# Interleaving the high and low parts of the up weights and moving the activations to another byte offset in a one-core hybrid decoder layer

## The chip, the cores and the metric

The kernel runs on one NeuronCore of a Trainium2 chip. The metric is the device time of one execution in microseconds (us). The core has a matrix engine (TensorE, PE in the profile, its weight loads PEld), VectorE (DVE), ScalarE (ACT), GpSimd (POOL) and a queue that issues transfers (SP). They share a memory of 128 partitions, SBUF; TensorE writes into eight banks of a second one, PSUM.

## The reference, cut to what matters

```python
h = rms_norm(x, mix_norm)
z = h @ w_in                           # q, k, v, r, gate of group A; q, k, v of group B
o_gla = silu(gr) * rms_norm(gla_chunked(gq, gk, gv, log_a), gla_norm)
o_swa = swa_sink_attention(sq, sk, sv, sinks)
x = x + concat([o_gla, o_swa]) @ w_out
h2 = rms_norm(x, ffn_norm)
u = causal_dwconv(h2 @ w_up, conv_w, conv_b)       # 3 taps along the sequence
a, b = split(u, 2)
x = x + (silu(a) * b) @ w_down
```

Sequence and model width are 1,024, the inner width of the feed-forward part is 2,816. All is float32.

## The kernel before, in words

**Precision.** A float32 matrix is split into a high part `hi`, rounded to the format of TensorE's fast float32 mode, and a low part `lo = x - hi`. A product is three fast matmuls: high by high, high by low, low by high (`PASSES`, line 30). `split` (line 95) makes the parts: ScalarE copies the high part, and GpSimd or VectorE subtracts it from the source for the low part. A matmul takes a stationary operand of 128 columns (the weight load) and streams a moving operand of up to 512 columns against it.

**Tiles.** `big` (line 65) holds the transposed activations, high and low: 65,536 bytes in each partition. In the dense stage it is the stationary operand, in the up stage the moving one. Its order before is half of the sequence, block of 128 features `k`, part `r`, row block within the half, row: `rows(t, ks, r)` takes the rows of one block `t`, and `b_operand` (line 810) takes all 512 rows of a half, which then lie in one run of 2,048 bytes. `ex` (line 667) holds three sums of activations in the same way. Weights lie in slots of 4,096 bytes (`slot_tile`, line 85), high part in the first 2,048 bytes, low part in the second.

**Stages.** First come five dense products with `w_in` (`dq`, `dk`, `dv`, `dg`, `dr`) with the attention work between them, then the product with `w_out` (`do`); `dense` (line 323) issues 24 matmuls for a row block (eight blocks of features, three passes), except that `unit_q_part` (line 710) issues those of the first three `dq` row blocks in pieces. Then the feed-forward part runs over 22 chunks of 128 inner columns. Each chunk makes seven up products P1 to P7 of a Strassen-like scheme (`product`, line 830), 12 matmuls each: the weights are the stationary operand, `big` (P1, P2, P3, P5) or `ex` (P4, P6, P7) the moving one. `up_operand` (line 788) makes the weights of each, `post` the convolution taps and the gate, and between the up products run the down products of the chunk pair before (`down_pair`, line 1014), whose two operands both lie in slots.

**Order.** A list of events with due times, written out by hand at the end of the function, sets the order of the program; each engine works through its own queue in that order. Weights of an up product are made two products ahead.

**Where the tiles lie.** The memory map of this kernel gives, in bytes of each partition: `big` from 1,152, `cc` (convolution constants, 704 bytes) from 66,688, three raw buffers from 67,392, `acc` from 79,680, `ex` from 112,448. From the other end: `mhalf` (96 bytes) from 229,248, nine slots below it from 192,384 on, 4,096 bytes apart. Small tiles take a multiple of 32 bytes.

Of the kernel before, what the change touches and what calls it, by code (L numbers as in the profile page):

```python
# [9 lines left out]
F32 = mybir.dt.float32  # L10
F32R = mybir.dt.float32r
# [6 lines left out]
P = 128  # L18
T = 1024
D = 1024  # L20
NT = T // P
KD = D // P
# [12 lines left out]
def hymba_layer_kernel(ctx, tc, x, mix_norm, w_in, w_alpha2, b_alpha, gla_norm,  # L35
# [3 lines left out]
    act, dve, pool, pe, sp = nc.scalar, nc.vector, nc.gpsimd, nc.tensor, nc.sync  # L39
# [10 lines left out]
    base = ctx.enter_context(tc.tile_pool(name="base", bufs=1))  # L50
# [4 lines left out]
    def bank(name):  # L55
        ps["n"] += 1
        if "f" in ps:
            return ps["f"][2 + ps["n"] % 2]

        for start, which in (("n2pt_6", "b"), ("do1_7", "a"), ("n2pt_3", "a")):  # L60
            if name.startswith(start):
                return ps[which].tile([P, 512], F32, tag="b", name=name)
        return ps["ab"[ps["n"] % 2]].tile([P, 512], F32, tag="b", name=name)

    big = base.tile([P, 2, KD, 2, 4, P], F32R, name="big")

    def rows(t, ks, r):
        return big[:, t // 4, ks, r, t % 4, :]

    RAW_BUFS, K4, K2, N_WARM = 3, 6, 5, 5  # L70

# [1 line left out]
        return base.tile([P, 1024], F32, tag="raw", name=name, bufs=RAW_BUFS)  # L73

    edge = ctx.enter_context(tc.tile_pool(name="edge", bufs=1, side="right"))
    mhalf = edge.tile([P, 24], F32, name="mhalf")
    w_keep = ctx.enter_context(tc.tile_pool(name="wa", bufs=1, side="right"))
    w_late = {}
    swp = ExitStack()
# [5 lines left out]
    def slot_tile(slot, name, dt=F32R):  # L85
        return w_keep.tile([P, 2, 512], dt, tag=f"w{slot}", name=name, bufs=1)
# [8 lines left out]
    def split(src, hi, lo, eng=None, hi_eng=None):  # L95
        if hi_eng is None:
            act.copy(hi, src)  # L97
        else:
            hi_eng.tensor_copy(hi, src)
        (eng or pool).tensor_sub(lo, src, hi.bitcast(F32))  # L100
# [126 lines left out]
    def norm2_sums(t):  # L227

        i, ex, pn = t - 4, fin["ex"], fin["pn"]
        p0, p1 = fin["pb", t]  # L230

        def put(src, hi, lo):
            split(src, hi, lo, dve)

        def extra(n):
            return ex[:, n, :, 0, i, :], ex[:, n, :, 1, i, :]

        def own(ks):
            return rows(t, ks, 0), rows(t, ks, 1)

        b12 = pn.tile([P, 4, P], F32, tag="b12", name=f"b12_{t}", bufs=1)
        b11, b21 = ([rows(i, ks, r).bitcast(F32) for r in range(2)] for ks in (slice(0, 4), slice(4, 8)))
        act.copy(b12, p0)
        put(p1, *own(slice(4, 8)))
        dve.tensor_sub(p0, p0, b11[0])
        dve.tensor_sub(p0, p0, b11[1])
        put(p0, *own(slice(0, 4)))
        dve.tensor_sub(p1, p1, b12)
        put(p1, *extra(1))
        dve.tensor_add(p1, p1, b11[0])  # L250
        dve.tensor_add(p1, p1, b11[1])
        put(p1, *extra(0))
        dve.tensor_sub(p0, b21[0], p1)
        dve.tensor_add(p0, p0, b21[1])
        put(p0, *extra(2))

    trs = {}

    def tr_hi(t, q, h, tag):
        pt = bank(f"{tag}pt_{t}_{q}")  # L260
        for k in range(4):
            c = (q * 4 + k) * P
            pe.transpose(pt[:, k * P:(k + 1) * P], h[:, c:c + P], ident)
        trs[tag, t, q] = pt.rearrange("p (k c) -> p k c", k=4)
        act.copy(rows(t, slice(q * 4, q * 4 + 4), 0), trs[tag, t, q])

    def tr_lo(t, q, tag):
        hi, lo = (rows(t, slice(q * 4, q * 4 + 4), r) for r in range(2))
        dve.tensor_sub(lo, trs[tag, t, q], hi.bitcast(F32))

    def norm_tr(t, h, tag):
# [5 lines left out]
    blocks = {}  # L277
# [45 lines left out]
    def dense(t, ws, n, name):  # L323
        pb = bank(name)
        for k in range(KD):
            for i, (ra, rb) in enumerate(PASSES):
                pe.matmul(pb[:, :n], lhsT=rows(t, k, ra), rhs=ws[k][:, rb, :n],  # L327
                          start=(k == 0 and i == 0), stop=(k == KD - 1 and i == 2))
        return pb

# [299 lines left out]
    def gate_tr(t, gs):  # L630
        pb = bank(f"ogt{t}")
        for h in range(4):
            pe.transpose(pb[:, h * P:(h + 1) * P], gs[:, h * P:(h + 1) * P], ident)
        pv = pb.rearrange("p (h c) -> p h c", h=4)
        hi, lo = (rows(t, slice(0, 4), r) for r in range(2))
        act.activation(hi, pv, AF.Copy, scale=glan)
        dve.scalar_tensor_tensor(lo, pv, glan, hi.bitcast(F32), op0=ALU.mult, op1=ALU.subtract)
        src = qo[:, t, :].rearrange("p (j c) -> p j c", j=4)
        hi, lo = (rows(t, slice(4, 8), r) for r in range(2))
        split(src, hi, lo)  # L640


    fin = {}
# [19 lines left out]
    def open_norm2():  # L663
        st.close()
        w_late["pool"] = swp.enter_context(tc.tile_pool(name="wb", bufs=1, side="right"))
        xp = ctx.enter_context(tc.tile_pool(name="xp", bufs=1))
        fin["ex"] = xp.tile([P, 3, 4, 2, 4, P], F32R, name="ex")
        fin["sn"] = ExitStack()
        pn = fin["pn"] = fin["sn"].enter_context(tc.tile_pool(name="pn", bufs=1))
        ffn = fin["ffn"] = pn.tile([P, D], F32, name="ffn")  # L670
        sp.dma_start(ffn, ffn_norm.partition_broadcast(P).rearrange("p o d -> p (o d)"))
        fin["s1"] = pn.tile([P, 4, P], F32, name="s1_0")
# [18 lines left out]
    psb = {}  # L691
# [18 lines left out]
    def unit_q_part(t, k0, k1):  # L710
        if k0 == 0:
            psb["q", t] = bank(f"dq{t}")
        pb = psb["q", t]
        for k in range(k0, k1):

            for i, (ra, rb) in enumerate(((0, 0), (1, 0), (0, 1))):
                pe.matmul(pb, lhsT=rows(t, k, ra), rhs=blocks["q"][k][:, rb, :],  # L717
                          start=(k == 0 and i == 0), stop=(k == KD - 1 and i == 2))

    def q_done(t):  # L720
# [2 lines left out]
    def unit_q(t):  # L723
        q_post(t, dense(t, blocks["q"], 512, f"dq{t}"))

    def unit_k(t):
        kvl_post(t, dense(t, blocks["k"], 272, f"dk{t}"))

    def unit_v(t):
        act.activation(vg[0][:, t, :], dense(t, blocks["v"], 512, f"dv{t}"), AF.Copy, scale=row_scale(t))  # L730
# [14 lines left out]
        if half == 1:  # L745
            norm2_stat(t)


    cc = base.tile([P, 4, 44], F32, name="cc")

    def conv_cols():
        cr = k2_tile("cr")[:44, :].rearrange("p (j c) -> p j c", j=4)
# [24 lines left out]
    def sums(s1, a11, a21, a22, eng=pool):  # L777
        eng.tensor_add(s1, a21, a22)
        eng.tensor_sub(a21, a11, a21)
        eng.tensor_sub(a11, s1, a11)  # L780
# [7 lines left out]
    def up_operand(ch, name):  # L788
        ra, rb = raws["u", ch, 0], raws.get(("u", ch, 1), raws["u", ch, 0])
        a11, a12, a21, a22 = ra[:, 0:4], ra[:, 4:8], rb[:, 0:4], rb[:, 4:8]  # L790
        src = {"A11": a11, "A12": a12, "A21": a21, "A22": a22, "S2": a11, "S3": a21,
               "S4": a11 if ch else a12}.get(name)
        if name == "S2" and ch:
            s1 = psb["S1", ch] = fin["ff"].tile([P, 4, P], F32, tag="s", name=f"S1_{ch}", bufs=1)
            sums(s1, a11, a21, a22)
        elif name == "S1":
            src = psb["S1", ch]
        elif name == "S4" and ch:
            pool.tensor_sub(a11, a12, a11)
        slot = U_SLOT.get((ch, name))  # L800
        if slot is None:
            slot = 1 + -turn[0] % 3
            turn[0] += 1
            U_SLOT[ch, name] = slot
        w = fin["pn"].tile([P, 2, 512], F32R, name=f"{name}w_{ch}") if slot < 0 else slot_tile(slot, f"{name}w_{ch}")
        w = w.rearrange("p r (k n) -> p r k n", k=4)
        split(src, w[:, 0], w[:, 1], dve if ch < 2 and name[1] == "1" and name[0] == "A" else None)
        blocks["u", ch, name] = w

    def b_operand(name, k, r):  # L810
        ex = fin["ex"]
        return {"B11": big[:, 0, k, r], "B21": big[:, 0, 4 + k, r],
                "B22": big[:, 1, 4 + k, r], "T1": big[:, 1, k, r],
                "T2": ex[:, 0, k, r], "T3": ex[:, 1, k, r], "T4": ex[:, 2, k, r]}[name]

    PROD = {"P1": ("A11", "B11"), "P2": ("A12", "B21"), "P3": ("S4", "B22"), "P4": ("A22", "T4"),
            "P5": ("S1", "T1"), "P6": ("S2", "T2"), "P7": ("S3", "T3")}
# [77 lines left out]
        act.copy(dst, pb)  # L895

    def save_edge(ch, key, pb):
        e = psb[key, ch] = fin["ff"].tile([P, 2], F32, tag="e", name=f"{key}_{ch}", bufs=2)
        act.copy(e, pb[:, 510:512])

    def c11(ch):
        pb = psb["P2", ch]
        dve.tensor_add(pb, psb["p1", ch], pb)
        ua = psb["ua", ch] = wide_tile(f"ua{ch}", "ua")
        conv(ch, 0, ua, pb, 0, 512, True)
        save_edge(ch, "e", pb)
# [191 lines left out]
    for c in halves:  # L1098
        split(mix_row[:, c], mix_hl[0][0:1, c], mix_hl[1][0:1, c], dve)
        pb = bank(f"mix{len(mix_ps)}")  # L1100
# [119 lines left out]
    for ch, i, name in order:  # L1220
# [7 lines left out]
        if ch < 2 or (ch, i) == (2, 0):  # L1228
            n = 0
        elif ch < L - 1 or (ch, i) == (L - 1, 0):  # L1230
            n = 1
        else:
            n = 2
# [24 lines left out]
    for p in range(NPAIR):  # L1258
        for k in range(7):

            n = 7 * p + k - 2
# [51 lines left out]
```

## Time and profile before

| what | value |
|---|---|
| median of 3 runs | 1039.2 us (1038.97 to 1039.4) |
| the profiled execution | 1039.1 us |
| its span, first to last instruction | 1037.4 us |
| granted TensorE clock | 1.000 |
| busy: PE, DVE, ACT, POOL | 99%, 76%, 46%, 60% |
| the chain that ended last | PE 97% |

The profile is one execution recorded by the hardware. A group row of it names line, engine, operation, what it writes and reads (`out<-in`), shape and count, then busy time in us, the mean duration in ns, and the idle time before with what ended it. A timeline row has its start and its length in us, then the same names and the count of equal instructions that it merges. A row of the windows view has, after the stretch, the busy time and count of PE, PEld, DVE, ACT and POOL, then the granted clock and the transfers. Matmuls are pipelined, so a single one's duration is longer than the step from one to the next.

### The profile page before, as it was taken

How to read it: one execution, taken by the hardware profiler on the slowest of the kernel's cores; microseconds unless marked ns; L12 is line 12 of the kernel's file. 1: busy time of each engine (PE TensorE's matmuls, PEld its weight loads, DVE VectorE, ACT ScalarE, POOL GpSimd, SP SyncE). 2: the span in 40 equal slices, each digit the busy share in tenths (PEclk: the TensorE clock that was granted, in tenths of full speed). 3: DMA queues.
4: the chain of work that ended last, by engine and by line, in shares of the span. 5: the costliest groups of instructions: out<-in, count | busy, mean ns of one | idle time of the engine just before them, and what ended most of it. 6: DMA issues, size and time to landing. Idle time of an engine off the chain costs nothing.

```text
span 1037.4 us, 13921 instructions
## 1 busy us (share of the span) xinstructions
PE 1030.0 (99%) x4976; PEld 849.3 (82%) x4976; DVE 793.4 (76%) x1332; ACT 480.6 (46%) x988; POOL 618.4 (60%) x510
## 2 busy tenths in 40 slices
PE   9999999999999999999999999999999999999998
PEld 6899887888888888888888888888888888888887
DVE  6776667755131699887979899897979798998976
ACT  5627655445340446554444445444444444454441
POOL 4592132325550205867868787877778787978750
PEclk9999999999999999999999999999999999999999
DMA  6152113002044202112120111222121211121104
GB/s 217 61 154 62 45 50 93 21 1 82 1 122 163 61 1 82 41 41 82 41 81 26 57 45 57 61 62 62 41 82 41 62 41 47 55 62 61 41 21 162
DMA packets 67502, 67.13 MB, mean 65 GB/s; under 512 B 4648, under 2 KB 52201, under 8 KB 67434
## 3 DMA queue, kind: packets, MB, share of 16 engines
q1 hardware_dynamic: 63448, 61.27, 18.9%
q10 hardware_dynamic: 3986, 4.99, 2.0%
q8 instruction: 39, 0.64, 0.2%
q14 instruction: 29, 0.24, 0.1%
HBM read 57.33 MB, written 4.19 MB: 59 GB/s over the span
## 4 chain that ended last, share of the span: by engine, by line
PE 97%; DMA 1%; DVE 1%; ACT 0%; issue 0%; POOL 0%; DVEq 0%; ACTq 0%; SPq 0%
PE fb L843 39%; PE dn_P L1024 18%; PE do L327 8%; PE dr L327 4%; PE dg L327 4%; PE dv L327 4%; PE dq L327 3%; PE dk L327 2%; PE gb L843 2%; PE dq L717 1%; PE pv L500 1%; PE fb L1053 1%; PE dl L1053 1%; PE go L610 1%; PE ga L601 1%; PE sc L453 1%
## 5 line engine op out<-in xcount | busy, mean ns | idle before, releaser
L1028 DVE TENSOR_TENSOR acc<-acc,dn_P 128x1024 f32<-128x1024 f32 x140 | 169.9, 1215 | 61.5 <-PE dn_P L1024 60.3
L1024 PE MATMUL dn_P<-dw,dg 128*128 128x512 f32 x840 | 214.0, 390 | 0.0
L1024 PEld LDWEIGHTS dn_P<-dw,dg 128*128 128x128 f32 x840 | 157.6, 188 | 34.5
L327 PE MATMUL do<-wow,big 128*128 128x512 f32 x384 | 90.9, 393 | 0.0
L100 POOL TENSOR_TENSOR dw<-dn,dw 128x512 fp32r<-128x512 f32 x50 | 68.8, 1376 | 25.3 <-ACT dw L97 24.1
L327 PEld LDWEIGHTS do<-wow,big 128*128 128x128 f32 x384 | 71.1, 188 | 14.4
L895 ACT COPY ca<-fb 128x512 f32<-128x512 f32 x62 | 36.3, 586 | 68.2 <-PE fb L843 68.2
L843 PE MATMUL fb<-ex,S2w 128*128 128x512 f32 x252 | 62.5, 394 | 0.0
L843 PE MATMUL fb<-ex,S3w 128*128 128x512 f32 x252 | 62.5, 394 | 0.0
L850 DVE SCALAR_TENSOR_TENSOR ua<-fb,cc,ua 128x511 f32<-128x511 f32 x84 | 62.2, 741 | 0.3
L843 PE MATMUL fb<-ex,A22w 128*128 128x512 f32 x252 | 62.2, 394 | 0.0
L843 PE MATMUL fb<-big,A11w 128*128 128x512 f32 x252 | 61.2, 389 | 0.0
L843 PE MATMUL fb<-big,S1w 128*128 128x512 f32 x252 | 61.1, 389 | 0.0
L843 PE MATMUL fb<-big,S4w 128*128 128x512 f32 x252 | 61.1, 389 | 0.0
L843 PE MATMUL fb<-big,A12w 128*128 128x512 f32 x252 | 60.9, 390 | 0.0
L843 PEld LDWEIGHTS fb<-ex,S2w 128*128 128x128 f32 x252 | 47.2, 187 | 11.3
L843 PEld LDWEIGHTS fb<-ex,A22w 128*128 128x128 f32 x252 | 47.2, 187 | 11.3
L843 PEld LDWEIGHTS fb<-ex,S3w 128*128 128x128 f32 x252 | 47.2, 187 | 11.3
L843 PEld LDWEIGHTS fb<-big,S1w 128*128 128x128 f32 x252 | 47.3, 188 | 10.0
L843 PEld LDWEIGHTS fb<-big,A11w 128*128 128x128 f32 x252 | 47.3, 188 | 10.0
L843 PEld LDWEIGHTS fb<-big,S4w 128*128 128x128 f32 x252 | 47.3, 188 | 10.0
L843 PEld LDWEIGHTS fb<-big,A12w 128*128 128x128 f32 x252 | 47.2, 188 | 9.8
(432 smaller groups left out, 2392.1 us busy)
## 6 DMA issues: line engine op xcount, KB each, us to landing
up<-in_w_up_dram SPq DMA_DIRECT2D x44, 512.0 KB, 3.8
dn<-in_w_down_dram SPq DMA_DIRECT2D x22, 512.0 KB, 3.5
acc<-in_x_dram SPq DMA_DIRECT2D x8, 512.0 KB, 6.5
out_dram<-acc SPq DMA_DIRECT2D x15, 256.0 KB, 2.0
xt<-in_x_dram SPq DMA_DIRECT2D x7, 512.0 KB, 3.2
vraw<-in_w_in_dram SPq DMA_DIRECT2D x4, 512.0 KB, 3.9
graw<-in_w_in_dram SPq DMA_DIRECT2D x4, 512.0 KB, 3.7
qt<-qt ACTq DMA_DIRECT2D x16, 128.0 KB, 2.2
```

What stands on the lines that cost most here:

```text
L100: (eng or pool).tensor_sub(lo, src, hi.bitcast(F32))
L327: pe.matmul(pb[:, :n], lhsT=rows(t, k, ra), rhs=ws[k][:, rb, :n], start=(k == 0 and i == 0), stop=(k == KD - 1 and i == 2))
L453: pe.matmul(pbs[-1][:, j % 2, :], lhsT=ql[:, g, qc], rhs=kt[:, g, kc], start=False, stop=True)
L500: pe.matmul(pbs[i][HALF[g]], lhsT=vv[rows, t - 1 + b, HALF[g]], rhs=rhs[rows, :, HALF[i]], start=start, stop=stop)
L601: pe.matmul(pb[:, pr * 256:(pr + 1) * 256], lhsT=gqt[t][:, pr, :], rhs=qbd[t % 2][:, pr], start=(pr == 0), stop=(pr == 1))
L610: pe.matmul(pb[:, h * P:(h + 1) * P], lhsT=asb[:, h, :], rhs=v[:, h * P:(h + 1) * P], start=(h == 0), stop=(t == 0 and h == 3))
L843: pe.matmul(pb, lhsT=w[:, ra, k, :], rhs=b_operand(bn, k, rb), start=(onto is None and i == 0), stop=(i == 11), skip_group_check=onto is n ...
L850: dve.scalar_tensor_tensor(dst, src, w, dst, op0=ALU.mult, op1=ALU.add)
L895: act.copy(dst, pb)
L1024: pe.matmul(pb[:, i], lhsT=g[:, ra, c:c + P], rhs=w[:, rb, :], start=(onto is None and n == 0), stop=(n == 2), skip_group_check=onto is no ...
L1028: dve.tensor_add(acc, acc, pb)
L1053: pe.matmul(pb[:, c0:c1], lhsT=g[:, ra, (t % 4) * P:(t % 4 + 1) * P], rhs=w[:, rb, c0:c1], start=(ch == NCH - 2 and i == 0), stop=(ch == N ...
```

## The change

`big` and `ex` get a new order: row block first, then feature block, part, row. Rows of one block are now together, and the 512 rows of a half that an up product streams lie in four runs of 512 bytes, 8,192 bytes apart in `big` and 4,096 in `ex`. The weights of the up products alternate within their slot, one word high, one word low, so a weight load reads every second word. `cc` is allocated ahead of `big`, `mhalf` shrinks from 24 to 8 columns, and the small edge tiles `e` (two of 32 bytes) move from the pool `ff` into `base`, behind the raw buffers. `norm2_sums` is written for the new order with the same operations. The weights of the dense and the down products keep their layout.

```diff
-    big = base.tile([P, 2, KD, 2, 4, P], F32R, name="big")
-
-    def rows(t, ks, r):
-        return big[:, t // 4, ks, r, t % 4, :]
+    cc = base.tile([P, 4, 44], F32, name="cc")
+    big = base.tile([P, NT, KD, 2, P], F32R, name="big")
...
-    mhalf = edge.tile([P, 24], F32, name="mhalf")
+    mhalf = edge.tile([P, 8], F32, name="mhalf")
...
-        act.copy(rows(t, slice(q * 4, q * 4 + 4), 0), trs[tag, t, q])
+        act.copy(big[:, t, q * 4:q * 4 + 4, 0, :], trs[tag, t, q])
...
-                pe.matmul(pb[:, :n], lhsT=rows(t, k, ra), rhs=ws[k][:, rb, :n],
+                pe.matmul(pb[:, :n], lhsT=big[:, t, k, ra, :], rhs=ws[k][:, rb, :n],
...
-        fin["ex"] = xp.tile([P, 3, 4, 2, 4, P], F32R, name="ex")
+        fin["ex"] = xp.tile([P, 3, 4, 4, 2, P], F32R, name="ex")
...
-    cc = base.tile([P, 4, 44], F32, name="cc")
...
-        w = w.rearrange("p r (k n) -> p r k n", k=4)
+        w = w.rearrange("p a c -> p (a c)").rearrange("p (k n r) -> p r k n", k=4, r=2)
         split(src, w[:, 0], w[:, 1], dve if ch < 2 and name[1] == "1" and name[0] == "A" else None)
...
-        return {"B11": big[:, 0, k, r], "B21": big[:, 0, 4 + k, r],
-                "B22": big[:, 1, 4 + k, r], "T1": big[:, 1, k, r],
-                "T2": ex[:, 0, k, r], "T3": ex[:, 1, k, r], "T4": ex[:, 2, k, r]}[name]
+        return {"B11": big[:, 0:4, k, r, :], "B21": big[:, 0:4, 4 + k, r, :],
+                "B22": big[:, 4:8, 4 + k, r, :], "T1": big[:, 4:8, k, r, :],
+                "T2": ex[:, 0, :, k, r, :], "T3": ex[:, 1, :, k, r, :],
+                "T4": ex[:, 2, :, k, r, :]}[name]
...
-        e = psb[key, ch] = fin["ff"].tile([P, 2], F32, tag="e", name=f"{key}_{ch}", bufs=2)
+        e = psb[key, ch] = base.tile([P, 2], F32, tag="e", name=f"{key}_{ch}", bufs=2)
```

More of the change, by code (lines that the diff above doesn't have):

```diff
@@ L230, in norm2_sums, with put @@
         p0, p1 = fin["pb", t]
[L232 to L239, printed above, removed]
+        def put(src, dst):
+            split(src, dst[:, :, 0, :], dst[:, :, 1, :], dve)
         b12 = pn.tile([P, 4, P], F32, tag="b12", name=f"b12_{t}", bufs=1)
-        b11, b21 = ([rows(i, ks, r).bitcast(F32) for r in range(2)] for ks in (slice(0, 4), slice(4, 8)))
+        b11, b21 = big[:, i, 0:4].bitcast(F32), big[:, i, 4:8].bitcast(F32)
         act.copy(b12, p0)
[L244 to L247, printed above, removed]
+        put(p1, big[:, t, 4:8])
+        dve.tensor_sub(p0, p0, b11[:, :, 0, :])
+        dve.tensor_sub(p0, p0, b11[:, :, 1, :])
+        put(p0, big[:, t, 0:4])
         dve.tensor_sub(p1, p1, b12)
[L249 to L255, printed above, removed]
+        put(p1, ex[:, 1, i])
+        dve.tensor_add(p1, p1, b11[:, :, 0, :])
+        dve.tensor_add(p1, p1, b11[:, :, 1, :])
+        put(p1, ex[:, 0, i])
+        dve.tensor_sub(p0, b21[:, :, 0, :], p1)
+        dve.tensor_add(p0, p0, b21[:, :, 1, :])
+        put(p0, ex[:, 2, i])
     trs = {}
@@ L264, in tr_hi @@
         trs[tag, t, q] = pt.rearrange("p (k c) -> p k c", k=4)
-        act.copy(rows(t, slice(q * 4, q * 4 + 4), 0), trs[tag, t, q])
+        act.copy(big[:, t, q * 4:q * 4 + 4, 0, :], trs[tag, t, q])
     def tr_lo(t, q, tag):
-        hi, lo = (rows(t, slice(q * 4, q * 4 + 4), r) for r in range(2))
+        hi, lo = big[:, t, q * 4:q * 4 + 4, 0, :], big[:, t, q * 4:q * 4 + 4, 1, :]
         dve.tensor_sub(lo, trs[tag, t, q], hi.bitcast(F32))
@@ L634, in gate_tr @@
         pv = pb.rearrange("p (h c) -> p h c", h=4)
-        hi, lo = (rows(t, slice(0, 4), r) for r in range(2))
+        hi, lo = big[:, t, 0:4, 0, :], big[:, t, 0:4, 1, :]
         act.activation(hi, pv, AF.Copy, scale=glan)
@@ L638, in gate_tr @@
         src = qo[:, t, :].rearrange("p (j c) -> p j c", j=4)
-        hi, lo = (rows(t, slice(4, 8), r) for r in range(2))
+        hi, lo = big[:, t, 4:8, 0, :], big[:, t, 4:8, 1, :]
         split(src, hi, lo)
@@ L716, in unit_q_part @@
             for i, (ra, rb) in enumerate(((0, 0), (1, 0), (0, 1))):
-                pe.matmul(pb, lhsT=rows(t, k, ra), rhs=blocks["q"][k][:, rb, :],
+                pe.matmul(pb, lhsT=big[:, t, k, ra, :], rhs=blocks["q"][k][:, rb, :],
                           start=(k == 0 and i == 0), stop=(k == KD - 1 and i == 2))
```

## The prediction

> **What bounds the kernel now.** I read the page first: the busy table, then the chain of work that ended last.
>
> ```profile
> span 1037.4 us, 13921 instructions
> PE 1030.0 (99%) x4976; PEld 849.3 (82%) x4976; DVE 793.4 (76%) x1332; ACT 480.6 (46%) x988; POOL 618.4 (60%) x510
> PE 97%; DMA 1%; DVE 1%; ACT 0%; issue 0%; POOL 0%; DVEq 0%; ACTq 0%; SPq 0%
> ```
>
> TensorE is busy for 99% of the span and carries 97% of the chain. It waits for nobody to speak of, so only a shorter step from one matmul to the next can make the kernel much faster. The profiled execution took 1039.1 us, 1.7 us more than its span; the median of the three runs is 1039.2, so sums made against 1039.1 hold for the median as well.
>
> The groups by line give the counts and the duration of a single matmul, the timeline gives runs of equal matmuls.
>
> ```profile
> L1024 PE MATMUL dn_P<-dw,dg 128*128 128x512 f32 x840 | 214.0, 390 | 0.0
> L327 PE MATMUL do<-wow,big 128*128 128x512 f32 x384 | 90.9, 393 | 0.0
> L843 PE MATMUL fb<-ex,S2w 128*128 128x512 f32 x252 | 62.5, 394 | 0.0
> L843 PE MATMUL fb<-ex,A22w 128*128 128x512 f32 x252 | 62.2, 394 | 0.0
> L843 PE MATMUL fb<-big,A11w 128*128 128x512 f32 x252 | 61.2, 389 | 0.0
> L843 PE MATMUL fb<-big,S1w 128*128 128x512 f32 x252 | 61.1, 389 | 0.0
> L843 PE MATMUL fb<-big,A12w 128*128 128x512 f32 x252 | 60.9, 390 | 0.0
> L327 PE MATMUL dv<-vw,big 128*128 128x512 f32 x192 | 46.5, 395 | 0.0
> L327 PE MATMUL dq<-qw,big 128*128 128x512 f32 x120 | 28.6, 394 | 0.0
> L717 PE MATMUL dq<-qw,big 128*128 128x512 f32 x72 | 19.3, 406 | 0.6 <-POOL qw L305 0.3 <-DVE big L269 0.2
> L843 PE MATMUL gb<-ex,S2w 128*128 128x512 f32 x12 | 3.2, 404 | 0.0
> ```
>
> ```profile
> 613.24 1.52 PE L1024 MATMUL dn_P<-dw,dg 128*128 128x512 f32 x6
> 614.60 2.96 PE L843 MATMUL fb<-ex,S2w 128*128 128x512 f32 x12
> 617.40 1.54 PE L1024 MATMUL dn_P<-dw,dg 128*128 128x512 f32 x6
> 618.78 2.88 PE L843 MATMUL fb<-big,S1w 128*128 128x512 f32 x12
> 344.73 7.64 PE L327 MATMUL do<-wow,big 128*128 128x512 f32 x33
> ```
>
> A run lasts (count - 1) steps and one full duration. So a step is (2.88 - 0.389) / 11 = 226.5 ns where the up product streams `big`, and (2.96 - 0.394) / 11 = 233.3 ns where it streams `ex`. The down products step by 226 to 230 ns (1.52 and 1.54 us for six), the dense ones by (7.64 - 0.393) / 32 = 226.5 ns. All are the same instruction: 128 weight columns, 512 moving columns. What differs is where the operands lie. In the memory map of this kernel `big` starts at byte 1,152 of a partition, the weight slots at 192,384 and every 4,096 after it, `ex` at 112,448; modulo 256 that is 128, 128 and 64. Distance 0 goes with 226.5, distance 64 with 233.3.
>
> How short could a step be? Two operations bound it.
>
> ```profile
> L601 PE MATMUL ga<-qbd,gkt 128*128 128x256 f32 x32 | 8.5, 389 | 0.0
> 246.76 1.03 PE L601 MATMUL ga<-qbd,gkt 128*128 128x256 f32 x4
> L263 PE MATMUL n1pt<-ident,h 128*128 128x128 f32 x64 | 8.8, 272 | 0.0
> 35.74 1.03 PE L263 MATMUL n1pt<-ident,h 128*128 128x128 f32 x8
> ```
>
> Plain float32 `ga` streams 256 columns, slowly, in (1.03 - 0.389) / 3 = 214 ns, give or take 2 for rounding. At that length 256 columns go at 1.2 columns a nanosecond, so a fast stream of 512 at twice that speed needs the same 213 ns (an estimate). The transposes, with 128 columns each, step by (1.03 - 0.272) / 7 = 108 ns: one weight load of 128 columns takes no less than that and hides under a 512-column stream. I take 215 ns as the step of a stream that loses nothing. The up products then lose 11.5 and 18.3 ns a matmul today, and since only the distance of the operands tells them apart, I take it that the weight reads and the moving reads hinder each other in SBUF.
>
> The Trainium skill speaks against that reading: "SBUF — State Buffer", Who interferes with whom, gives TensorE two independent read ports and says that it never waits on anyone. By that rule no placement matters and the sum is 0. The trace disagrees, with 226.5 against 233.3 ns.
>
> **The change, part by part.**
>
> *Interleaved weights.* A weight load reads 512 contiguous bytes in 108 ns, 4.7 bytes a ns; the moving operand reads 2,048 bytes in 215 ns, 9.5 bytes a ns. One stream therefore sweeps past the other, and meets it at every distance. With high and low parts alternating, a load steps 8 bytes a column and runs through 1,024 bytes in the same time: 9.5 bytes a ns, as fast as the moving operand. Two streams at one speed keep their distance. If they start apart they never meet; if they start together they block each other until one has slipped by. `ga`, whose moving operand advances 4.8 bytes a ns (1,024 in 214 ns) and whose weights go at 4.7, is the one row with equal speeds, and it loses nothing, though its demand is also half as large. Bounds: 215 ns below; above, twice today's loss, should a load that opens twice as many lines cost twice as much. I take 215, the row with equal speeds.
>
> Counts: 252 matmuls in each of seven products from the rows, plus 12 each in the first chunk (the `gb` row): 264. Four products stream `big`, 1,056 matmuls; three stream `ex`, 792. Gain: 1,056 x 11.5 ns = 12.1 us and 792 x 18.3 ns = 14.5 us, together 26.6 us.
>
> *Placement.* `cc` (704 bytes) now precedes `big`, which moves to 1,856; `mhalf` falls from 96 to 32 bytes, so the slots move up 64, to 192,448; the two 32-byte edge tiles in `base` push `ex` to 112,512. Modulo 256: 64, 192, 128. `big` is 128 from the slots, as the words say. `ex` stays 64 away: that part of the activations is not 128 off. The down products read slot against slot and stay at distance 0: nothing changes there.
>
> The dense products pay or gain here, for they keep contiguous weights, read from `big`, and stream the slots. They are 384 + 4 x 192 = 1,152 matmuls with 512 columns (`dv`, `dg`, `dr` and `dq` of 192 each; `dq` as 120 + 72). Distance 128 is not in the trace for warm streams of this length. Bounds: the 215 ns floor (a gain of 13.2 us) and 233.3, the worst other distance (a loss of 1,152 x 6.8 ns = 7.8 us). I take the loss, from the only row of a distance that is not 0. `dk`, 192 matmuls of 272 columns, streams rows of 1,088 bytes, so its distances are mixed before and after: 0.
>
> *The four-piece moving operand.* An up product's 512 columns are now four runs of 512 bytes, 8,192 or 4,096 bytes apart, both multiples of 256; the phase runs on. 0, with one ns a matmul (1.8 us) as the outer bound either way.
>
> *Strided writes.* The high parts are written by ScalarE and the low parts, except the first chunks' `A11` and `A12`, by GpSimd, now every 8 bytes.
>
> ```profile
> 400.00:1037.00 637.00, 633.88 (x2776) 518.74 (x2774) 550.31 (x709) 295.79 (x503) 470.38 (x345) 1.00 0.19 58
> 600.00:700.00 100.00, 100.00 (x438) 81.94 (x437) 91.44 (x116) 47.12 (x79) 80.67 (x59) 1.00 0.17 52
> L100 POOL TENSOR_TENSOR S3w<-up,S3w 128x512 fp32r<-128x512 f32 x22 | 33.0, 1501 | 20.2 <-ACT S3w L97 20.2
> L100 POOL TENSOR_TENSOR A12w<-up,A12w 128x512 fp32r<-128x512 f32 x20 | 26.0, 1299 | 0.0
> L97 ACT CAST A22w<-up 128x512 fp32r<-128x512 f32 x22 | 13.8, 626 | 4.7 <-PE fb L843 3.0 <-PE gb L843 1.6
> ```
>
> The window rows give PE, PEld, DVE, ACT and POOL in that order. GpSimd makes seven such groups in the up stage, 26.0 to 33.0 us each, some 204 us of its 470.4 in 637. ScalarE has seven of about 13 us; doubled, they would bring it from 46% to 61%, still hidden. GpSimd takes 2.5 ns an element (1,299 / 512), slow enough that I expect the step not to show: 0. The cover is 167 us of idle GpSimd; in the densest stretch it is 19.3 of 100 us, so there it ends when the strided group takes 1.6 times as long (204 / 637 x 100 = 32 us, and 19.3 / 32 = 0.6).
>
> *What is late next.* VectorE is busy 91.44 of 100 us in that stretch. A stage that is 26.6 of 637 us (4%) shorter raises that to 95%. TensorE's PSUM banks wait behind VectorE, so I add 2 us, between 0 and 6.
>
> *The rest* (sums rewritten over whole tiles, `rows` gone) leaves the same instructions with the same shapes: 0.
>
> Sum: -26.6 + 7.8 + 2 = -16.8; 1039.1 - 16.8 = 1022.3, say 1022 us. Its own range: 1012.5 (no loss in the dense part, none on VectorE) to 1032 (up steps of 220 ns, 9.2 us more).
>
> **The rivals.**
>
> *One kind gains alone* (13%). `ex` keeps distance 64, `big` gets 128; one may keep apart and the other meet. With `big` alone: 1039.1 - 12.1 + 7.8 = 1034.8; with `ex` alone: 1032.4. For it: the new distances differ.
>
> *The dense part gains too* (8%): distance 128 may be best for contiguous reads. Up to 13.2 instead of -7.8: 999 to 1012. Against it: the only two distances with steady runs today are both lossy.
>
> *No effect* (8%): the loss belongs to the fast stream itself, or gain and dense loss cancel, 1039. Against it: 226.5 and 233.3 for one shape. It is also where the Trainium skill's independent ports (the section above) would leave the time.
>
> *Slower: the streams lock in collision* (17%). Equal speed works both ways: if load and stream start in the same group of lines they stay there, and a load that touches twice the lines loses twice. At today's loss doubled: +26.6 + 7.8 = 1073.5; with the up part unchanged and the dense loss alone, 1047. It decides from an up step over 226.5 and 233.3. For it: the start of a load against its stream is not in the trace. Against it: blocking shifts the two apart, and equal speed then keeps them apart.
>
> *Slower: GpSimd becomes the bound* (7%), from 1.6 times on in the densest stretch; at twice, 470.4 + 204 = 675 us against 637: +38, 1077. The Trainium skill has a rule for this: "Vector Engine (DVE) Microarchitecture Reference", Measured stream behaviour on trn2, keeps the full rate only for runs of two adjacent words, and gives 1.71 to 2.51 ns a column in place of 1.05 for single words. Its "SBUF — State Buffer", Specifications, asks only two hits in a line of 16 bytes, which a step of 8 bytes has. No stepped write is in this trace to judge between them.
>
> **How the numbers follow.** The forecast itself has 47%. Faster is 47 + 13 + 8 = 68%, the same 8%, slower 17 + 7 = 24%, with 0.2% (2 us) as about what a measurement here can tell from no change. The range is 1010 to 1047: from just under the forecast's own lower end to the dense loss without any gain; outside are most of the dense gain and the two heavy slowdowns.
>
> **What would show it.** A run of 12 up matmuls on `big` would last 2.75 us and on `ex` the same, against 2.88 and 2.96; the `do` run of 33 would last 7.86 us; down runs of six stay at 1.52 to 1.54. The GpSimd rows of the up weights stay under 1.6 us and the ScalarE rows under 0.7. The mechanism is wrong if up runs do not shorten, or if they lengthen together; if they shorten and the time does not, look for idle time ahead of TensorE released by DVE or POOL.

## The result, and the profile after

The changed kernel takes 1048.45 us (median of 4 runs, 1047.6 to 1048.83) against 1039.28 for the kernel before: a ratio of 1.0088, 95% interval 1.007 to 1.0105. It is slower by 9.2 us. The forecast was 1022 us, with a range of 1010 to 1047.

The page of the kernel after: span, busy table and chain.

```profile
span 1045.9 us, 13921 instructions
PE 1038.9 (99%) x4976; PEld 863.5 (83%) x4976; DVE 799.3 (76%) x1332; ACT 486.6 (47%) x988; POOL 621.4 (59%) x510
PE 98%; DVE 1%; ACT 0%; DMA 0%; POOL 0%; issue 0%; ACTq 0%; SPq 0%
```

The same instructions run, and TensorE still waits for nobody. Its busy time grew by 8.9 us, the span by 8.5: the matmuls themselves step more slowly. The groups by line of the kernel after (line numbers are up to nine lower than before):

```profile
L1015 PE MATMUL dn_P<-dw,dg 128*128 128x512 f32 x840 | 216.0, 392 | 0.0
L319 PE MATMUL do<-wow,big 128*128 128x512 f32 x384 | 92.6, 397 | 0.0
L834 PE MATMUL fb<-big,S1w 128*128 128x512 f32 x252 | 62.2, 393 | 0.0
L834 PE MATMUL fb<-ex,S2w 128*128 128x512 f32 x252 | 61.7, 392 | 0.0
```

The busy column (the figure ahead of the mean duration) gives the loss by product. The four groups of up products on `big` (`S1w` is one of them) take 4.4 us more than before and the three on `ex` 2.3 us less; the dense products with 512 columns take 4.8 us more (`do` alone 1.7) and the down products, whose operands did not move, 2.0 more. Together that is 8.9 us, the whole growth of TensorE's busy time. The mean durations move the same way: +4 ns on `big`, -2 on `ex`, +4 for `do`, +2 for the down products.

The timeline of the kernel after shows the steps:

```profile
620.12 2.92 PE L834 MATMUL fb<-ex,S2w 128*128 128x512 f32 x12
622.88 1.54 PE L1015 MATMUL dn_P<-dw,dg 128*128 128x512 f32 x6
624.27 2.94 PE L834 MATMUL fb<-big,S1w 128*128 128x512 f32 x12
627.04 1.54 PE L1015 MATMUL dn_P<-dw,dg 128*128 128x512 f32 x6
339.81 18.98 PE L319 MATMUL do<-wow,big 128*128 128x512 f32 x81
```

On `ex` a step is (2.92 - 0.392) / 11 = 230 ns, on `big` (2.94 - 0.393) / 11 = 231.5, in the dense stage (18.98 - 0.397) / 80 = 232.3. Nothing is near the 215 ns of the forecast. An undivided down run of six now lasts 1.54 or 1.55 us everywhere. Before, it lasted 1.52 behind a product on `big` (77 of 78 runs) and 1.54 behind one on `ex` (all 54). The start times in the trace of before show where the difference lies: behind `big` every step of such a run is 226 or 227 ns, behind `ex` the steps are 225, 236, 229, 232, 231 and 227. So a run starts out of the rhythm that the product ahead of it leaves, and takes its six matmuls to come back to the fast one.

The other engines do not set the end: the chain is TensorE's for 98%. These are groups of the kernel after that write or load interleaved weights; the last two lines are of the kernel before:

```profile
L98 POOL TENSOR_TENSOR A12w<-up,A12w 128x512 fp32r<-128x512 f32 x20 | 26.4, 1319 | 0.0
L95 ACT CAST A22w<-up 128x512 fp32r<-128x512 f32 x22 | 14.6, 666 | 4.7 <-PE fb L834 3.1 <-PE gb L834 1.6
L98 DVE TENSOR_TENSOR A11w<-up,A11w 128x512 fp32r<-128x512 f32 x2 | 1.4, 689 | 0.6 <-ACT A11w L95 0.6
L834 PEld LDWEIGHTS fb<-big,S4w 128*128 128x128 f32 x252 | 49.3, 196 | 9.1
L100 DVE TENSOR_TENSOR A11w<-up,A11w 128x512 fp32r<-128x512 f32 x2 | 1.4, 690 | 0.7 <-ACT A11w L97 0.7
L843 PEld LDWEIGHTS fb<-big,S4w 128*128 128x128 f32 x252 | 47.3, 188 | 10.0
```

GpSimd goes from 1,299 to 1,319 ns and ScalarE from 626 to 666; VectorE, which writes the low parts of `A11` and `A12` in the first two chunks, stays at 690. The weight load, 188 ns before, records 196.

### The profile page after: what moved, and what is told of

It reads as the page before. It is cut to its first block, busy times and chain, and to the rows that moved or that the text cites. A ratio compares the mean times of both kernels' runs of the same rounds, so it can differ in the third digit from the quotient of the medians.

```text
span 1045.9 us, 13921 instructions
## 1 busy us (share of the span) xinstructions
PE 1038.9 (99%) x4976; PEld 863.5 (83%) x4976; DVE 799.3 (76%) x1332; ACT 486.6 (47%) x988; POOL 621.4 (59%) x510
## 4 chain that ended last, share of the span: by engine, by line
PE 98%; DVE 1%; ACT 0%; DMA 0%; POOL 0%; issue 0%; ACTq 0%; SPq 0%
PE fb L834 39%; PE dn_P L1015 19%; PE do L319 9%; PE dg L319 4%; PE dr L319 4%; PE dv L319 4%; PE dq L319 3%; PE dk L319 2%; PE gb L834 2%; PE dq L709 1%; PE pv L492 1%; PE dl L1044 1%; PE fb L1044 1%; PE go L602 1%; PE ga L593 1%; PE sc L444 1%
```

## The experiments

After this result there were three theories. Theory 1: the distance between the operands modulo 256 sets the step, and 128 is a bad distance for contiguous reads. Theory 2: the 8-byte step of the weight load costs the up products. Theory 3: the four pieces of the moving operand cost. The first three kernels below separate the parts; the fourth applies theory 1 to the kernel before. "Distance" is always meant modulo 256 bytes.

**The placement alone** (kernel before; contiguous weights, old order of `big`):

```diff
+    cc = base.tile([P, 4, 44], F32, name="cc")
     big = base.tile([P, 2, KD, 2, 4, P], F32R, name="big")
...
-    mhalf = edge.tile([P, 24], F32, name="mhalf")
+    mhalf = edge.tile([P, 8], F32, name="mhalf")
...
-    cc = base.tile([P, 4, 44], F32, name="cc")
...
-        e = psb[key, ch] = fin["ff"].tile([P, 2], F32, tag="e", name=f"{key}_{ch}", bufs=2)
+        e = psb[key, ch] = base.tile([P, 2], F32, tag="e", name=f"{key}_{ch}", bufs=2)
```

> The placement of the change alone: weights contiguous, activations in their old order, big 128 bytes off the slots, ex 64 off. Theory 1 (the distance modulo 256 sets the step, and distance 128 is a bad one for contiguous reads): dense steps about 232.5 ns as after the change, up steps on big as bad as that (232 to 233, against 226.9 before), on ex unchanged at 233.3, down steps about 230.5; dense +5, up on big +6, down +2: about 1052 us. Theory 2 (the 8-byte step of the weight load is what costs the up products): dense 232.5, up on big 227, ex 233.3, down 228: about 1044 us. Theory 3 (the four pieces of the moving operand cost): as theory 2.

Measured: 1050.75 us, ratio 1.0112 (1.0097 to 1.0127). Groups:

```profile
L1024 PE MATMUL dn_P<-dw,dg 128*128 128x512 f32 x840 | 215.3, 392 | 0.0
L328 PE MATMUL do<-wow,big 128*128 128x512 f32 x384 | 92.6, 397 | 0.0
L843 PE MATMUL fb<-big,S1w 128*128 128x512 f32 x252 | 62.5, 394 | 0.0
L843 PE MATMUL fb<-ex,S2w 128*128 128x512 f32 x252 | 62.5, 394 | 0.0
```

In mean duration, distance 128 costs the dense products 4 ns each, as in the changed kernel, and the up products on `big` 5 (389 to 394). `ex` kept its distance and its 394. That is theory 1's reading; theories 2 and 3 had `big` at 389.

**The interleaving alone** (kernel before, all tiles at their old places):

```diff
-        w = w.rearrange("p r (k n) -> p r k n", k=4)
+        w = w.rearrange("p a c -> p (a c)").rearrange("p (k n r) -> p r k n", k=4, r=2)
```

> The interleaving alone: old order of the activations, old places (big at distance 0, ex at 64). Theory 1: up steps on big stay at 227 or fall, ex falls to 230 as after the change, dense stays at 228: 1036 us or less. Theory 2: up on big about 231.4 and ex 230.3 as after the change, down 230.5: 1039.2 + 4.7 - 2.4 + 2.1, about 1044 us. Weight loads of the up products 194 to 196 ns by both, if that lengthening comes from the 8-byte step.

Measured: 1043.96 us, ratio 1.0047 (1.0032 to 1.0062).

```profile
L843 PE MATMUL fb<-big,S1w 128*128 128x512 f32 x252 | 62.6, 394 | 0.0
L843 PE MATMUL fb<-ex,S2w 128*128 128x512 f32 x252 | 61.8, 392 | 0.0
L843 PEld LDWEIGHTS fb<-ex,S2w 128*128 128x128 f32 x252 | 49.0, 194 | 9.1
L843 PEld LDWEIGHTS fb<-big,S1w 128*128 128x128 f32 x252 | 48.7, 193 | 10.0
```

So theory 2 holds too, with an addition: interleaving costs 5 ns of duration at distance 0 (389 to 394) and gains 2 at distance 64 (394 to 392). The weight loads lengthen at both distances, so the longer load alone does not set the sign.

**The new order of the activations alone** (changed kernel, with `cc`, `mhalf`, `e` and the line of the weights as before):

```diff
-        w = w.rearrange("p a c -> p (a c)").rearrange("p (k n r) -> p r k n", k=4, r=2)
+        w = w.rearrange("p r (k n) -> p r k n", k=4)
```

> The new order of the activations alone: moving operand in four runs of 512 bytes, contiguous weights, old places. Theories 1 and 2: every step as before, 1039 us. Theory 3: up steps on big move from 226.9 to about 231, on ex from 233.3 to 230, 1042 us or more.

Measured: 1038.94 us, ratio 0.9997 (0.9987 to 1.0006).

```profile
L834 PE MATMUL fb<-big,S1w 128*128 128x512 f32 x252 | 61.1, 389 | 0.0
L834 PE MATMUL fb<-ex,S2w 128*128 128x512 f32 x252 | 62.5, 394 | 0.0
```

Both are as before, so theory 3 falls.

**The kernel before with `ex` at distance 0:**

```diff
-        e = psb[key, ch] = fin["ff"].tile([P, 2], F32, tag="e", name=f"{key}_{ch}", bufs=2)
+        e = psb[key, ch] = base.tile([P, 2], F32, tag="e", name=f"{key}_{ch}", bufs=2)
```

> The kernel before with one edit: the edge tiles e in base, which moves ex by 64 bytes, so that big, ex and the slots all lie at distance 0. Theory 1: up steps on ex fall from 233.3 to 226.9 (792 x 6.4 ns = 5.1 us), and the down products behind them from 230 to 227 (420 x 3 ns = 1.3 us): about 1033 us, faster than both kernels. Rival (the sums in ex are slow for another reason, not their place): 1039 us.

Measured: 1033.1 us, ratio 0.9943 (0.9927 to 0.996): the fastest kernel of the study, by moving one tile by 64 bytes. Its timeline:

```profile
619.68 2.88 PE L843 MATMUL fb<-ex,S3w 128*128 128x512 f32 x12
622.40 1.52 PE L1024 MATMUL dn_P<-dw,dg 128*128 128x512 f32 x6
623.76 2.88 PE L843 MATMUL fb<-big,S4w 128*128 128x512 f32 x12
626.48 1.52 PE L1024 MATMUL dn_P<-dw,dg 128*128 128x512 f32 x6
```

Both kinds of up product now take 2.88 us, and the down runs behind either 1.52.

**The changed kernel with every distance at 0:**

```diff
-    cc = base.tile([P, 4, 44], F32, name="cc")
     big = base.tile([P, NT, KD, 2, P], F32R, name="big")
+    cc = base.tile([P, 4, 44], F32, name="cc")
...
-    mhalf = edge.tile([P, 8], F32, name="mhalf")
+    mhalf = edge.tile([P, 24], F32, name="mhalf")
```

> The changed kernel with every distance at 0: cc behind big and mhalf of 24 columns again, the edge tiles stay in base; interleaving and new order stay. Theory 1: big and ex now behave alike, and the dense part is back at 228. Theory 2 and theory 4, from the run of the interleaving alone: up steps 233.2 on big and on ex alike, down 230 or less, dense 228: 1033 + 1848 x 6.5 ns + 1 to 2, about 1046 us. If the interleaving were harmless here, 1033.

Measured: 1045.3 us, ratio 1.0058 (1.0041 to 1.0075).

```profile
L834 PE MATMUL fb<-big,S1w 128*128 128x512 f32 x252 | 62.7, 394 | 0.0
L834 PE MATMUL fb<-ex,S2w 128*128 128x512 f32 x252 | 62.5, 394 | 0.0
```

Both kinds of up product show 394 ns, `do` is back at 393. Interleaving is not harmless at distance 0: with every distance at 0 and contiguous weights, the kernel above took 1033.1 us.

**The disputed step by itself.** The last two kernels send sequences of equal matmuls, without the layer around them. Each was run once, at a granted clock of 1.000:

```python
def run(name, dist, step=1, cols=P, n=512, count=32):
    pb = ps.tile([P, 512], F32, tag="b", name=name)
    for i in range(count):
        m0 = 64 + (i % 2) * 512
        w0 = 64 + (i % 3) * 512 - dist // 4
        pe.matmul(pb[:cols, :n], lhsT=wt[:, w0:w0 + step * cols:step], rhs=mv[:, m0:m0 + n],
                  start=(i == 0), stop=(i == count - 1))
```

> Not the layer: x is copied to the output, and beside it TensorE runs sequences of 32 equal matmuls of 512 columns, one sequence for each layout of the weights (contiguous, every second word, every fourth word, 64 instead of 128 columns) and each distance modulo 256 between moving operand and weights; everything twice. Contiguous: 226.7 ns at distance 0, 233 at 192, about 232.5 at 128, by every theory that goes by distance. Every second word, theory 1 as the prediction had it (equal speed keeps two streams apart): about 215 ns at some distances and over 235 at others. Theory 4, formed on the first four runs (a stepped load opens twice the lines, so load and stream meet at every distance): 230 to 234 at all distances, weight loads of 193 to 196 ns. 64 columns: if the loss above 215 ns belongs to the weight load it halves, to about 221 at distance 0; if it belongs to the stream, 226.7 stays. Every fourth word: theory 4 gives a longer load again (over 200 ns) and a step of 235 or more; theory 1 gives no rule.

In its timeline the names end in a letter for the distance, counted from the weights up to the moving operand: a 0, c 32, e 64, i 128, m 192 bytes. In the layer `ex` lies 64 bytes below the slots, so its place there is the sweep's m. `cont` has contiguous weights, `two` every second word, `four` every fourth, `halfcols` 64 columns.

```profile
44.40 7.17 PE L60 MATMUL conte<-mv,wt 128*128 128x512 f32 x30
140.48 7.52 PE L60 MATMUL twom<-mv,wt 128*128 128x512 f32 x32
184.88 15.48 PE L60 MATMUL fouri<-mv,wt 128*128 128x512 f32 x64
222.36 7.53 PE L60 MATMUL halfcolsa<-mv,wt 128*64 128x512 f32 x32
251.88 7.58 PE L60 MATMUL twoi<-mv,wt 128*128 128x512 f32 x32
289.11 7.63 PE L60 MATMUL twoa<-mv,wt 128*128 128x512 f32 x32
304.04 7.63 PE L60 MATMUL contm<-mv,wt 128*128 128x512 f32 x32
318.99 7.59 PE L60 MATMUL conti<-mv,wt 128*128 128x512 f32 x32
333.89 7.49 PE L60 MATMUL conte<-mv,wt 128*128 128x512 f32 x32
341.22 7.63 PE L60 MATMUL contc<-mv,wt 128*128 128x512 f32 x32
356.02 7.43 PE L60 MATMUL conta<-mv,wt 128*128 128x512 f32 x32
```

A run of 32 is 31 steps and one duration of about 0.39 us. Contiguous weights: 227 ns at distance 0, 233.5 at 32, 232.3 at 128, 233.5 at 192. Every second word: 233.5 at 0, 231.9 at 128, 230 at 192. These are the steps of the layer: 226.5 on `big` and 233.3 on `ex` before, 231.5 and 230 after, 232.3 in the dense stage after. So place and layout of the two operands are enough to make them, and nothing else in the layer is needed.

The interleaved steps lie between 230 and 236 over the nine distances tried, with nothing near 215, so the equal-speed picture fails, and theory 4 comes close (it had said 230 to 234). Distance 64 (`conte`) gave 229.0 in this pass (7.49 us) and 233.8 in the first (7.17 us for 30 matmuls): the same sequence has more than one rhythm. A load of 64 columns, shorter by 54 ns, does not shorten the step at distance 0 (230.3 against 227.1). So the loss above 215 is not in proportion to the time for which a load runs beside the stream. The groups of the same kernel show the loads:

```profile
L60 PEld LDWEIGHTS fouri<-mv,wt 128*128 128x128 f32 x64 | 15.4, 310 | 0.0
L60 PEld LDWEIGHTS twoi<-mv,wt 128*128 128x128 f32 x64 | 12.5, 196 | 2.3
L60 PEld LDWEIGHTS conti<-mv,wt 128*128 128x128 f32 x64 | 12.0, 188 | 2.8
L60 PEld LDWEIGHTS halfcolsi<-mv,wt 128*64 128x64 f32 x64 | 8.6, 134 | 6.0
```

Theory 4 had said of a step of 16 bytes: loads over 200 ns, 235 or more a matmul. They record 310, and the step is (15.48 - 0.40) / 63 = 239 ns at distance 128 and 235 at distance 0.

> Again sequences of 32 equal matmuls beside a copy of x to the output, now over the length of the stream (256 to 512 columns, contiguous at distance 0 and 64, every second word at distance 0), the columns of the weight load (32, 96, 128) and distances that are no multiple of 16 bytes. Theory 1's picture, a stream that is hindered while a load runs beside it: the loss above N / 2.4 ns shrinks with the columns of the load, 32 columns leaving about 3 of 13 ns. Theory 5, formed on the first sweep (64 columns lose as much as 128): a cost for each matmul that neither length nor load size changes much, 11 to 14 ns above N / 2.4 at every N and with 32 columns too, and 17 to 20 with every second word. If instead the loss belongs to the stream's own reads, it grows with N: half at 256 columns.

Timeline of the last kernel: `len` varies the columns of the stream (e 256, g 384, h 448, i 512) at distance 0, `twolen` the same with every second word, `cols` the columns of the load (b 32).

```profile
37.37 6.36 PE L60 MATMUL lenh<-mv,wt 128*128 128x448 f32 x30
202.09 7.58 PE L60 MATMUL colsb<-mv,wt 128*32 128x512 f32 x32
209.50 7.62 PE L60 MATMUL twoleni<-mv,wt 128*128 128x512 f32 x32
216.97 6.67 PE L60 MATMUL twolenh<-mv,wt 128*128 128x448 f32 x32
223.47 5.71 PE L60 MATMUL twoleng<-mv,wt 128*128 128x384 f32 x32
233.72 3.99 PE L60 MATMUL twolene<-mv,wt 128*128 128x256 f32 x32
265.27 7.43 PE L60 MATMUL leni<-mv,wt 128*128 128x512 f32 x32
272.53 6.65 PE L60 MATMUL lenh<-mv,wt 128*128 128x448 f32 x32
279.02 5.73 PE L60 MATMUL leng<-mv,wt 128*128 128x384 f32 x32
289.28 3.99 PE L60 MATMUL lene<-mv,wt 128*128 128x256 f32 x32
```

With 0.28, 0.34 and 0.39 us for the last duration, the steps are 119.7 ns at 256 columns, 174 at 384 and 227 at 512. From 256 to 512 columns the step grows by 107.3 ns, which is 2.4 columns a nanosecond, so N columns take N / 2.4 ns of stream. Over that (106.7, 160, 213.3) the steps have 13, 14 and 14 ns: a cost for each matmul that is the same at these three lengths. The fourth breaks the rule: 448 columns take 207 ns in the first pass and 203 in the second, 20 and 16 over 186.7.

Nor does the cost shrink with the load, for 32 columns give (7.58 - 0.39) / 31 = 231.9 ns. That is the main point of theory 5; three of its numbers missed. The short load costs 18.6 ns and the 448 columns 16 to 20, not 11 to 14, and every second word costs 13 at 256 and 384 columns, 17 at 448 (no more than contiguous weights there) and 20 only at 512. So the extra cost of interleaving is no constant either; it belongs to this length and these places. The distances that are no multiple of 16 bytes show how fine the places are: contiguous weights take 227 ns at 4 bytes and 233 at 8 and at 12.

## Why the prediction was wrong, point by point

**The bound** was right: TensorE's step sets the end, and the time moved as its steps did.

**The step that failed** is the gain of the interleaving: "Two streams at one speed keep their distance. If they start apart they never meet", and with it "I take 215, the row with equal speeds". It stood for -26.6 us. Measured are steps of 231.5 and 230 ns: 4.4 us more on `big`, 2.3 less on `ex`, a net loss of 2.1. Split by part, the placement alone makes the kernel 11.4 us slower (1050.75), since distance 128 is bad for the up products with contiguous weights too; at these places the interleaving then brings back some 2.3 us (1048.45), a tenth of what it stood for. At distance 0 it costs: 4.6 us net in the kernel before, where only `big` lies there, and 12.2 us (1045.3 against 1033.1) where all does.

The runs showed that interleaved weights give 230 to 236 ns at all nine distances tried, and that shortening the load to 64 or 32 columns buys nothing at distance 0. The speeds were not at fault: an interleaved load records only 5 to 9 ns more than a contiguous one, so by the prediction's own measure load and stream were about as fast as each other, and still no step came near 215. The premise behind it, that today's loss is the time in which the two reads meet, is not borne out: at distance 0 some 13 ns of it stand at 256 columns as at 512, and a load of a quarter of the columns does not lower it. The row chosen as the floor, `ga`, was the wrong witness; it differs from the up products in format and speed, and the equal speed was my reading of it, not its cause. That it "loses nothing" was no finding either, for the floor of 215 was worked out from `ga` itself. The stream does take some 213 ns, by the slope over the lengths; but no run of 512 columns stepped faster than 226.5.

One reading behind that step was loose. The 108 ns of a load is the step of the transposes, and at the 1.2 columns a ns of `ga` their 128 streamed columns take 107 ns by themselves, so that row can only show that a load takes no more, not that it takes no less. The size holds all the same: loads of 128 and 64 columns record 188 and 134 ns, 54 ns for 64 columns.

**The dense loss** was right in sign and place, and too large: 6.8 ns a matmul forecast, 5.8 measured in a long run (226.5 to 232.3) and 4.2 over all of them, 4.8 us for 7.8. The experiment with the placement alone shows it without the interleaving.

**The distances** were right: `ex` stayed 64 away, and in the experiment with the placement alone it kept its 394 ns.

**The down products** were put at nothing because their operands do not move. They lost 2.4 ns each by the busy column, 2.0 us: the rhythm that an up product leaves carries over. The rows for this stood in the prediction, 1.52 behind `big` and 1.54 behind `ex`, and I read them as a spread.

**Four pieces, strided writes, VectorE**: four pieces cost nothing (0.9997). GpSimd's strided writes cost 20 ns of 1,299, ScalarE's 40 of 626, both hidden. "Vector Engine (DVE) Microarchitecture Reference" of the Trainium skill (Measured stream behaviour on trn2) gives single words 1.71 to 2.51 ns a column in place of 1.05. It speaks of VectorE, and for a step of 8 bytes the runs do not show it on any engine: VectorE took 689 ns for 690, ScalarE 1.06 times as long as before, GpSimd 1.02. The 2 us for a late VectorE were not put to the test, for the stage did not get shorter.

**The rivals.** "The streams lock in collision" named the right sign, but it was to decide from an up step over 226.5 and 233.3, and only the first came about: the step on `ex` fell to 230. Its price was nearly four times too high, and the runs do not bear out its mechanism; the case beside it, the up part unchanged and the dense loss alone, comes out at 1047 and is close by accident of the sum, since up and down products lost too and the dense part lost less. Of the others, "one kind gains alone" was right about `ex`, by 2.3 us where it had 14.5, but not that `big` stays as it was; "the dense part gains too" fell with the 232.3 ns of distance 128, "no effect" with the interval of the ratio, 1.007 to 1.0105, and GpSimd as the bound with its 1,319 ns.

What stays open: where the 13 ns come from, why contiguous weights at distance 0 get by with them at 512 columns, and why most other places cost 16 to 22. The runs show the steps, not what TensorE does in them.

## What to carry to other kernels

When TensorE is the bound and waits for nobody, compare the steps of equal matmuls by the tiles they read: a difference of a few ns between two tiles is worth more than reasoning about why, and moving the slower tile to the faster one's offset is the first thing to try (here one edit of 64 bytes, -6.2 us). Do not generalise from a distance that suits one layout of the weights to another, and count the products behind a changed one as touched. A mechanism that is to replace a measured optimum should be measured by itself, at two or three offsets, before the whole kernel is arranged around it.

## What the runs showed of the hardware that was not expected

- In the fast float32 mode a matmul with its weight load stepped by N / 2.4 ns (the slope worked out above) and a further 11 to 22, for N from 256 to 512, with 128 as with 32 columns in the load (a step of 16 bytes left aside). 227 ns was the shortest step of any sequence at 512 columns.
- The cost comes in lumps. Where the second half of a sequence keeps one step, alike to 1 ns by the start times in the traces, that step is 120.0, 146.7, 173.3 or 206.7 ns for 256, 320, 384 or 448 columns, and 226.7 or 233.3 ns for 512. That is 13.3 or 20.0 ns over N / 2.4, and all six are multiples of 6.67 ns. Other means come from sequences whose steps alternate, such as 226, 229 and 232 ns in `conte`. Why is not shown.
- The place of the operands matters to TensorE: 226.5 against 233.3 ns before, and the duration on `ex` falls from 394 to 389 ns when it is moved by 64 bytes. "SBUF — State Buffer" of the Trainium skill (Who interferes with whom) gives TensorE two independent read ports and has it wait for no one. That rule is about other engines; it names nothing by which the place of TensorE's own operands would matter, and here it does.
- A weight load with a step of 8 bytes records 193 to 197 ns in place of 188, one with 16 bytes 310. That agrees with "SBUF — State Buffer" of the Trainium skill (Specifications), which asks for two hits in a line of 16 bytes: a step of 8 bytes has two words in a line, a step of 16 bytes one.
- The rhythm of one product carries into the next: the same six down matmuls take 1.52 or 1.54 us by what ran ahead of them. In the last kernel the sequence with 512 columns, started behind one with 448, took nine matmuls to settle at 226.7 ns.
